# Attention scores of two heads on the two row halves of the array, heads built without doubled rows, weighted sums one block behind

## The chip, the cores and the metric

One Trainium2 core runs the whole program. The metric is device time in microseconds (us): the median of three runs of the kernel before is 1206.73 us (1206.26 to 1209.43).

## What is computed

A hybrid decoder layer on 1024 tokens of width 1024, all in float32. Half of the mixer's width is attention: 8 heads of 64 with RMS-normed queries and keys, three dilated causal windows whose outputs are merged by their softmax denominators. The other half is an S5 state-space mixer with a gated output. Both are normed, projected, added to `x`, and followed by a squared-ReLU MLP of width 4096.

```python
q = _rmsnorm(q, q_norm_g); k = _rmsnorm(k, k_norm_g)
attn = _dilated_attention(q, k, v).reshape(b, s, ATTN_WIDTH)   # 3 windows, merged
ssm = _s5_mixer(u, ...)
mix = concat([_rmsnorm(attn, attn_out_norm_g), _rmsnorm(ssm, ssm_out_norm_g)])
x = x + mix @ w_out
return x + square(relu(_rmsnorm(x, norm2_g) @ w_mlp_up)) @ w_mlp_down
```

The three windows are one softmax here: `bias` (128x1024) adds 8 ln(n) to a score that n windows see, and -1e30 to one that none sees.

## The kernel before, in words

TensorE multiplies fp32r operands. To keep float32 accuracy every operand is held as a rounded high part and the rest as a low part (`split`, L97; `split_scaled`, L101: ACT rounds, DVE subtracts), and a product is a sum of three: high by high, high by low, low by high (`mm3`, L120).

The program runs in this order. `project(0)` and `project(1)` (L219) make the rows of q and k, woven with the state-space mixer (`ssm_params`, `ssm_tables`, `ssm_main`) by the list at L674. Then come the values (`project(2)`), attention over 4 pairs of heads, the gate (`glu`, L712) and the mixer's half of the output projection (`out_ssm`, L786), all woven; then attention's half of the output projection (L834 on), and the MLP (`up_proj`, `down_proj`).

Places that the change and the steps below touch:

- `project` (L219): a row tile of q or k is 128 tokens by 8 heads by 2 copies of 64. ACT takes it from PSUM (L244), squares it into the place of the second copy (L245), DVE sums (L247), POOL forms the reciprocal root (L94, L95), DVE scales (L226), POOL makes the second copy (L227), and POOL's queue writes both copies to DRAM (`d_qk`, L228). Three such tiles rotate.
- `heads(p)` (L518) builds the operands of the pair p: it loads blocks of 512 tokens by 256 columns (`qk_r`, L525), transposes four 128x128 tiles per head and block (`pst`, L539) and evicts them. With the copies doubled, a transposed tile has the head's 64 rows twice, on partitions 0 to 63 and 64 to 127. For k the upper copy becomes the low part (L543, L544); for q the high part (`Qd[0]`) and the low part (`Qd[1]`) are each held twice.
- `scores(i, h)` (L567) takes query blocks 2i and 2i+1 of one head. Each block and each edge of at most 512 keys is two full-array products (L580), q high and q low against the stacked k, so it sums four terms. DVE adds the bias and takes the minimum (L582), ACT exponentiates (L585), DVE and POOL normalise (L587, L588).
- `weigh(i, h, P)` (L592) transposes the weights (`psp`, L603), splits them (`pt`, L606) and multiplies by the values (`mix`, L611). It runs one step behind the scores inside a pair; at a pair's end the last one runs without scores beside it (L647).
- `attn` (L564) yields costs, and `weave` (L649) interleaves two generators by the share of their stated totals; its other stream is `project(2)`, `glu`, `out_ssm` and the next pair's `heads`. What the weave emits is then scheduled, so that every engine has a fixed order.
- PSUM: three banks `s` (scores and `pst`), two `tr`, two `mm`, one `po`. One rotation of two SBUF buffers (`raw`) carries `qk_r`, `v_r`, the gate's and the output projection's weights.

Of the kernel before, what the change touches and what calls it, by code (L numbers as in the profile page):

```python
# [34 lines left out]
def hybrid_layer_kernel(ctx: ExitStack, tc: tile.TileContext, io: dict, out: bass.AP):  # L35
# [47 lines left out]
    d_qk = [dram.tile([T, 1024], F32, name=f"d_{n}") for n in "qk"]  # L83
# [89 lines left out]
    def kv_tiles(p):  # L173
        k, v, q0, q1 = (0, 1, 4, 5) if p % 2 else (6, 7, 8, 9)
        return (place(k, [128, 2, T], F32R, "K2"), [place(q, [128, 2, T], F32R, "Qd") for q in (q0, q1)],
                place(v, [128, 8, 2, 128], F32R, "V2"))
# [42 lines left out]
    def project(c):  # L219
# [3 lines left out]
        def scale(t, row, f):  # L223

            v, dup = row[:, :, 0], row[:, :, 1]
            tc.keep_in_program_order(DVE.tensor_tensor(v, v, f[:, :, None].to_broadcast([128, 8, 64]), op=OP.mult))  # L226
            POOL.tensor_scalar(dup, v, 1.0, 1.0, op0=OP.mult, op1=OP.mult)  # L227
            POOL.dma_start(out=d_qk[c][t * 128:(t + 1) * 128, :], in_=row.rearrange("p h a e -> p (h a e)"))  # L228

        w = [load_w(f"wq{c}_{i}", io["w_qkv"][c, :, 2 * i:2 * i + 2, :], 2, 512, g1, 2 * i) for i in range(4)]  # L230
        for t in ORDER[c]:
# [9 lines left out]
            if c < 2:  # L241
                row = sp2.tile([128, 8, 2, 64], F32, tag="rows", name="rows", bufs=3)
                v, sq = row[:, :, 0], row[:, :, 1]
# [274 lines left out]
    def heads(p, out_):  # L518
# [3 lines left out]
        def load():  # L522
            hf, c = todo.pop(0)
            st = rawp.tile([128, 1024], F32, tag="raw", name="qk_r").rearrange("p (t h e) -> p t h e", t=4, h=2)
            nc.sync.dma_start(out=st.rearrange("p t h e -> p t (h e)"),  # L525
                              in_=d_qk[c][hf * 512:hf * 512 + 512, 256 * p:256 * p + 256].rearrange("(t m) c -> m t c", m=128))
            return hf, c, st
# [3 lines left out]
        K2, Qd, V2 = kv_tiles(p)  # L531
        out_.update(K2=K2, Qd=Qd, V2=V2)
# [31 lines left out]
    def attn(p, K2, Qd, V2, rows=range(4)):  # L564
# [27 lines left out]
        def weigh(i, h, P):  # L592
# [42 lines left out]
            if h == 0:  # L635
                return
# [512 lines left out]
```

## Time and profile before

| what | value |
|---|---|
| median of three runs | 1206.73 us |
| the profiled execution's own time | 1207.53 us |
| its span | 1205.8 us |
| PE busy, of the span | 1131.7 us, 94% |
| DVE, ACT, POOL busy | 819.1, 574.9, 286.2 us |
| mean granted TensorE clock | 0.979 |

PE is TensorE's matmuls, PEld its weight loads. A busy share says only that an engine had something in it. What an engine waited for stands with the idle time ahead of an instruction, and the chain of waits follows the program back from its last instruction. A granted clock of 1.00 is 2.4 GHz, and 0.83 over 10 us means that a third of it ran at 1.2 GHz.

### The profile page before, as it was taken

To read this page: it belongs to the slowest core of one execution; us is meant where nothing else is said; L and a number is where in the kernel's file an instruction comes from. 1 tells how busy PE (TensorE), PEld (TensorE's weight loads), DVE (VectorE), ACT (ScalarE), POOL (GpSimd) and SP (SyncE) were. 2 spreads that over 40 slices of the span, in tenths; PEclk is the share of its full clock that TensorE was granted. 3 is DMA by queue.
4 is the path that set the end of the run, shared out by engine and by line. 5 is a ranking of instruction groups with operands and counts; after the bars stand their busy time and mean duration, and the time that the engine had idled before them with its cause. 6 is when DMAs were issued, how large, how long until landed. Compare 5 with 4: busy or idle time off the path is not lost.

```text
span 1205.8 us, 16171 instructions
## 1 busy us (share of the span) xinstructions
PE 1131.7 (94%) x5720; PEld 931.6 (77%) x5720; DVE 819.1 (68%) x1522; ACT 574.9 (48%) x979; POOL 286.2 (24%) x435
## 2 busy tenths in 40 slices
PE   5978989998999799999899999999999999999998
PEld 4756767787887587887778888888887888888887
DVE  6788886436787677767876666666656775576763
ACT  5432333445677456644555555555553434333332
POOL 4126654411344234333111212111110000000000
PEclk9989899999998899999899999999999999999999
DMA  7843262733433244454354434444399999566930
GB/s 266 330 144 92 90 230 108 249 114 100 141 124 114 94 148 152 141 168 158 122 185 160 159 139 162 155 155 150 123 344 396 386 387 344 190 229 197 324 142 35
DMA packets 112176, 224.49 MB, mean 186 GB/s; under 512 B 9440, under 2 KB 40160, under 8 KB 111072
## 3 DMA queue, kind: packets, MB, share of 16 engines
q1 hardware_dynamic: 92352, 157.31, 39.1%
q0 software_dynamic: 16576, 59.22, 12.8%
q10 hardware_dynamic: 3168, 6.93, 1.5%
q8 instruction: 45, 0.74, 0.2%
q14 instruction: 35, 0.29, 0.1%
HBM read 157.92 MB, written 65.50 MB: 185 GB/s over the span
## 4 chain that ended last, share of the span: by engine, by line
PE 69%; DVE 10%; DMA 10%; ACT 5%; POOL 3%; issue 2%; ACTq 0%; POOLq 0%; DVEq 0%; SPq 0%
PE psy L52 21%; PE psx L52 21%; PE pso L52 8%; PE psq L52 6%; PE psz L52 3%; PE pss L52 2%; PE psp L55 2%; DMA wm<-in_w_up_dram 2%; PE psg L52 2%; DMA wo_r<-in_w_o_dram 1%; PE psn L52 1%; POOL rsq L94 1%; DMA wq_r<-in_w_qkv_dram 1%; PE pst L55 1%; DMA raw<-in_w_down_dram 1%
## 5 line engine op out<-in xcount | busy, mean ns | idle before, releaser
L98 ACT ACTIVATE ud<-raw 128x1024 fp32r<-128x1024 f32 x112 | 112.9, 1053 | 186.0 <-PE psy L52 81.0
L99 DVE TENSOR_TENSOR ud<-raw,ud 128x1024 fp32r<-128x1024 f32 x112 | 132.6, 1221 | 80.2 <-ACT ud L98 80.2
L52 PE MATMUL psx<-X,wu 128*128 128x512 f32 (+1 forms) x780 | 183.0, 386 | 0.0
L52 PE MATMUL psy<-ud 128*128 128x512 f32 x768 | 174.6, 389 | 0.0
L52 PEld LDWEIGHTS psx<-X,wu 128*128 128x128 f32 x780 | 144.7, 188 | 30.2 <-DVE st L938 0.7
L52 PEld LDWEIGHTS psy<-ud 128*128 128x128 f32 x768 | 144.2, 188 | 29.9
L52 PE MATMUL psq<-wq,xt 128*128 128x512 f32 x576 | 146.9, 405 | 0.0
L52 PE MATMUL psx<-ud 128*128 128x512 f32 x576 | 131.5, 389 | 1.1 <-DVE ud L99 1.1
L52 PEld LDWEIGHTS psx<-ud 128*128 128x128 f32 x576 | 108.1, 188 | 23.9 <-DVE ud L99 1.6
L52 PEld LDWEIGHTS psq<-wq,xt 128*128 128x128 f32 x576 | 107.8, 193 | 23.0 <-issue 1.0
L52 PE MATMUL pso<-wo,mt 128*128 128x512 f32 x384 | 104.7, 413 | 5.1 <-ACT wo L102 3.4
L99 DVE TENSOR_TENSOR wu<-wm,wu 128x512 fp32r<-128x512 f32 x112 | 73.7, 687 | 30.4 <-ACT wu L98 30.3
L52 PE MATMUL psy<-X,wu 128*128 128x512 f32 x384 | 92.7, 389 | 0.6 <-ACT st L930 0.6
L98 ACT ACTIVATE wu<-wm 128x512 fp32r<-128x512 f32 x112 | 66.5, 626 | 53.0 <-DMA wm<-in_w_up_dram 26.3
L52 PEld LDWEIGHTS pso<-wo,mt 128*128 128x128 f32 x384 | 72.0, 196 | 21.6 <-ACT wo L102 4.6
L52 PEld LDWEIGHTS psy<-X,wu 128*128 128x128 f32 x384 | 71.8, 188 | 15.8 <-ACT st L930 1.0
L934 POOL DMA_DIRECT2D d_a<-st x80 | 43.2, 540 | 141.7 <-ACT st L940 70.7
L1039 DVE TENSOR_TENSOR raw<-raw 128x1024 f32<-128x1024 f32 x40 | 48.6, 1222 | 32.5 <-DMA raw<-in_w_down_dram 32.5
L588 POOL TENSOR_SCALAR s<-s,dn 128x128 f32<-128x128 f32 (+3 forms) x64 | 50.8, 796 | 70.0 <-DVE dn L587 64.0
L99 DVE TENSOR_TENSOR pt<-psp,pt 128x128 fp32r<-128x128 f32 (+2 forms) x96 | 51.3, 551 | 15.3 <-ACT pt L98 14.7
L52 PE MATMUL pso<-pt,V 128*128 128x256 f32 x320 | 57.6, 303 | 2.9 <-ACT pt L98 2.4
L52 PE MATMUL psu<-wu,xt 128*128 128x512 f32 x192 | 46.9, 404 | 12.3 <-ACT wu L102 8.1
(254 smaller groups left out, 1787.3 us busy)
## 6 DMA issues: line engine op xcount, KB each, us to landing
raw<-in_w_down_dram SPq DMA_DIRECT2D x96, 512.0 KB, 9.0
raw<-d_a SPq DMA_DIRECT2D x56, 512.0 KB, 7.8
d_a<-st POOLq DMA_DIRECT2D x80, 256.0 KB, 2.5
wm<-in_w_up_dram SPq DMA_DIRECT2D x32, 512.0 KB, 3.7
d_x<-x POOLq DMA_DIRECT2D x32, 256.0 KB, 2.6
d_a<-o POOLq DMA_DIRECT2D x32, 256.0 KB, 2.8
wq_r<-in_w_qkv_dram SPq DMA_DIRECT2D x12, 512.0 KB, 4.6
xr<-in_x_t_dram SPq DMA_DIRECT2D x8, 512.0 KB, 4.8
```

What stands on the lines that cost most here:

```text
L52: self.queued(nc.tensor.matmul(*a, **k))
L55: self.queued(nc.tensor.transpose(*a, **k))
L94: POOL.tensor_scalar(v[:, :n], in_, mul, EPS, op0=OP.mult, op1=OP.add)
L98: ACT.activation(h, src, AF.Copy)
L99: eng.tensor_tensor(l, src, h.bitcast(F32), op=OP.subtract)
L588: POOL.tensor_scalar(s[:, :n], s[:, :n], dn, 1.0, op0=OP.mult, op1=OP.mult)
L934: POOL.dma_start(out=d_a[blk // 2][i][blk % 2], in_=st)
L1039: DVE.tensor_tensor(rb, rb, raw_unit(wd(n, *b1)), op=op)
```

## The change

Rows of q and k are written to DRAM once, and POOL's copy is gone. `heads` loads 128 columns of a pair: a transposed tile then has head 0 on partitions 0 to 63 and head 1 on 64 to 127, and one `split_scaled` gives the high and low parts of both. A score product contracts over 64 partitions and uses one half of the array's rows; the two heads' products are issued in turn, into two PSUM banks, three for each head (high by high, high by low, low by high; low by low is gone). `scores` and `weigh` treat both heads of a row i; `weigh` runs a row behind, also across pairs (`carry`), and the pieces of the two are interleaved (`zipped`). Weights of the two heads rotate through four buffers in place of two, and a pair's heads wait until the pair before the last is over.

```diff
-    d_qk = [dram.tile([T, 1024], F32, name=f"d_{n}") for n in "qk"]
+    d_qk = [dram.tile([T, 512], F32, name=f"d_{n}") for n in "qk"]
...
-            v, dup = row[:, :, 0], row[:, :, 1]
+            v = row[:, 0]
             tc.keep_in_program_order(DVE.tensor_tensor(v, v, f[:, :, None].to_broadcast([128, 8, 64]), op=OP.mult))
-            POOL.tensor_scalar(dup, v, 1.0, 1.0, op0=OP.mult, op1=OP.mult)
-            POOL.dma_start(out=d_qk[c][t * 128:(t + 1) * 128, :], in_=row.rearrange("p h a e -> p (h a e)"))
+            POOL.dma_start(out=d_qk[c][t * 128:(t + 1) * 128, :], in_=v.rearrange("p h e -> p (h e)"))
...
-            for h in range(2):
-                pt = s_bank("pst")
-                for t in range(4):
-                    PE.transpose(pt[:, t * 128:t * 128 + 128], st[:, t, h], ident)
-                if c == 0:
-                    split_scaled(Qd[0][:, h, tt], Qd[1][:, h, tt], pt, gqk[:, 0:1])
-                else:
-                    ACT.activation(K2[:, h, tt], pt, AF.Copy, scale=gqk[:, 1:2])
-                    DVE.scalar_tensor_tensor(K2[64:128, h, tt], pt[64:128], gqk[64:128, 1:2],
-                                             K2[64:128, h, tt].bitcast(F32), op0=OP.mult, op1=OP.subtract)
+            pt = s_bank("pst")
+            for t in range(4):
+                PE.transpose(pt[:, t * 128:t * 128 + 128], st[:, t], ident)
+            to = K2 if c else Q2
+            split_scaled(to[:, 0, tt], to[:, 1, tt], pt, gqk[:, c:c + 1])
...
-                    ps = s_bank("pss")
-                    cw = max(256, c1 - c0)
-                    for a in range(2):
-                        PE.matmul(ps[:, :cw], lhsT=Qd[a][:, h, b * 128:(b + 1) * 128],
-                                  rhs=K2[:, h, c0:c0 + cw], start=a == 0, stop=a == 1)
+                ps = [s_bank("pss") for _ in range(2)]
+                cw = max(256, c1 - c0)
+                for aq, ak in ((0, 0), (0, 1), (1, 0)):
+                    for h, hp in enumerate(HALF):
+                        PE.matmul(ps[h][:, :cw], lhsT=Q2[hp, aq, b * 128:(b + 1) * 128], rhs=K2[hp, ak, c0:c0 + cw],
+                                  start=aq + ak == 0, stop=aq == 1)
...
+        for k0 in range(0, nb, 4):
+            kn = min(4, nb - k0)
+            for h in range(2):
+                pt = turn(k0, kn, h)
+                yield kn * 0.22
                 if pend:
                     mix(*pend)
-                    yield pend[1] * 0.213
-                pend = (k0, kn, pt)
+                    yield pend[1] * 0.238
+                pend = (k0, kn, h, pt)
...
         for i in rows:
-            for h in range(2):
-                P, cost = scores(i, h)
-                yield cost
-                if pend:
-                    yield from weigh(*pend)
-                pend = (i, h, P)
-        yield from weigh(*pend)
+            P = [place_turn((9, 0, 13, 14), [128, 2, T], F32, "s") for _ in range(2)]
+            yield from zipped(scores(i, P, K2, Q2), weigh(*carry.pop()) if carry else iter(()))
+            carry.append((p, i, P, V2))
```

The order on the engines, at three places.

PE, inside the rows 2 and 3 of the first pair of heads, before (`pss` scores, two products each):

```order
L52 MATMUL pss_2695<-K2_2217,Qd_2218 128x512
L52 MATMUL pss_2695<-K2_2217,Qd_2219 128x512
L52 MATMUL pss_2699<-K2_2217,Qd_2218 128x256
L52 MATMUL pss_2699<-K2_2217,Qd_2219 128x256
L52 MATMUL pss_2741<-K2_2217,Qd_2218 128x512
L52 MATMUL pss_2741<-K2_2217,Qd_2219 128x512
```

The same place of the changed kernel; here `pss_2701`, `pss_2745`, `pss_2776` are head 0 and `pss_2702`, `pss_2746`, `pss_2777` head 1 (`psp` and `pst` are transposes and `psg` products of the gate, all over the full array):

```order
L52 MATMUL pss_2701<-K2_2201,Q2_2202 128x512
L52 MATMUL pss_2702<-K2_2201,Q2_2202 128x512
L55 MATMUL psp_2812<-pack_66,s_2577 128x128 x4
L55 MATMUL pst_2721<-pack_66,qk_r_2575 128x128 x4
L52 MATMUL pss_2745<-K2_2201,Q2_2202 128x256 x3
L52 MATMUL pss_2746<-K2_2201,Q2_2202 128x256 x3
L52 MATMUL pss_2776<-K2_2201,Q2_2202 128x512 x3
L52 MATMUL psg_2608<-zs_2604,wg0_2593 128x256 x2
L52 MATMUL psg_2730<-zs_2604,wg0_2593 128x256 x2
L52 MATMUL pss_2777<-K2_2201,Q2_2202 128x512 x3
```

The scheduler has kept the two heads in turn for one group and drawn them apart in the next two, and full-array work stands between groups of half-array work. Through the whole order of the changed kernel, the 288 score products stand in 59 unbroken groups (36 of them of six); 117 times a product of one head is followed at once by one of the other, and 54 products have no such partner. Of the 59 groups 4 stand before the last product of the values' projection, 32 between it and the first product of the mixer's output weights, 23 behind that. By width the 117 are 56 of 512, 18 of 384 and 43 of 256 columns, the 54 are 31, 12 and 11.

PE at the first load of a pair, during the values' projection, before and after:

```order
L52 MATMUL psq<-wq_0_2172,xt 128x512 x6
L52 MATMUL psq<-wq_1_2179,xt 128x512 x6
L52 MATMUL psq<-wq_2_2186,xt 128x512 x6
L55 MATMUL pst<-pack,qk_r 128x128 x4
L52 MATMUL psq<-wq_3_2193,xt 128x512 x6
```

```order
L52 MATMUL psq<-wq_0_2156,xt 128x512 x6
L52 MATMUL psq<-wq_1_2163,xt 128x512 x6
L52 MATMUL psq<-wq_2_2170,xt 128x512 x2
L55 MATMUL pst<-pack,qk_r 128x128 x4
L52 MATMUL psq<-wq_2_2170,xt 128x512 x4
L52 MATMUL psq<-wq_3_2177,xt 128x512 x6
```

The first transposes of loaded rows stand four products earlier.

POOL in the first projection, before and after (`f` is a row's scale, `rows` its tile, `U` and `ga` belong to the state-space mixer):

```order
L94 TENSOR_SCALAR rsq<-f 128x8
L95 TENSOR_TENSOR f<-rsq,mhalf 128x8
L227 TENSOR_SCALAR rows<-rows 128x8x64
L228 DMA d_q<-rows 128x1024
L266 TENSOR_SCALAR U_1561<-U_1561 128x1024
L498 TENSOR_SCALAR ga<-ga 128x512 x2
```

```order
L94 TENSOR_SCALAR rsq<-f 128x8
L95 TENSOR_TENSOR f<-rsq,mhalf 128x8
L228 DMA d_q<-rows 128x512
L266 TENSOR_SCALAR U_1554<-U_1554 128x1024
L498 TENSOR_SCALAR ga<-ga 128x512 x2
```

The copy is gone and the write is half as wide; nothing else has moved.

## Rows read from the trace of the kernel before

**Rows 1.** Busy time by stretch, 95 to 515 us of the span: stretch, length, then busy us (instructions) of PE, PEld, DVE, ACT, POOL, the granted clock, the DMA share and GB/s.

```profile
95.00:229.50 134.50, 120.40 (x757) 95.66 (x757) 107.75 (x204) 48.92 (x74) 80.72 (x81) 0.97 0.41 137
229.50:283.00 53.50, 53.48 (x271) 44.97 (x272) 18.75 (x48) 21.27 (x47) 7.69 (x15) 0.97 0.40 139
283.00:396.00 113.00, 102.20 (x675) 88.26 (x675) 89.80 (x234) 78.08 (x174) 42.38 (x67) 0.94 0.39 125
396.00:415.00 19.00, 12.04 (x45) 7.22 (x44) 11.54 (x29) 9.95 (x21) 3.99 (x5) 0.87 0.35 111
415.00:515.00 100.00, 96.37 (x570) 81.19 (x569) 71.83 (x178) 57.57 (x120) 37.03 (x64) 0.99 0.45 143
```

**Rows 2.** What PE's weight loads waited for, 229.5 to 513.6 us: the waiting operation, who released it, us in total, times, longest.

```profile
PEld pso L52 <- ACT pt L98: 7.1, 16, 1.2
PEld psp L55 <- POOL s L588: 6.2, 11, 1.1
PEld pss L52 <- DVE mn L582: 5.5, 12, 0.9
PEld psp L55 <- DVE pt L99: 5.3, 7, 1.8
```

**Rows 3.** PE in order of time, runs of one kind: start us, us until the last one's end, engine, line, what, array rows*columns, shape, count.

```profile
129.47 7.10 PE L52 MATMUL psq<-wq,xt 128*128 128x512 f32 x30
136.41 0.61 PE L52 MATMUL psy<-D,U 128*128 128x128 f32 x4
...
310.39 1.60 PE L52 MATMUL pso<-pt,V 128*128 128x256 f32 x12
311.83 1.60 PE L52 MATMUL psg<-zs,wg 128*128 128x256 f32 x12
313.27 1.09 PE L52 MATMUL pss<-K,Qd 128*128 128x512 f32 x4
...
492.47 1.04 PE L55 MATMUL psp<-pack,s 128*128 128x128 f32 x8
```

**Rows 4.** The transposes of loaded rows and their evictions by tile (`pst`), whole span: duration in ns as least/median/most, first and last start, and how many of each shape.

```profile
L55 PE MATMUL pst<-pack,qk_r x128: 270/272/447, 229.5 to 452.5; 128*128 128x128 f32 x128
L102 ACT ACTIVATE Qd<-pst,pack x16: 677/687/702, 230.6 to 450.7; 128x512 fp32r<-128x512 f32 x16
L103 DVE SCALAR_TENSOR_TENSOR Qd<-pst,pack,Qd x16: 734/751/753, 231.4 to 451.6; 128x512 fp32r<-128x512 f32 x16
```

**Rows 5.** The score products and their evictions by tile (`pss`), whole span; columns as in Rows 4.

```profile
L52 PE MATMUL pss<-K,Qd x192: 274/390/775, 252.4 to 499.7; 128*128 128x512 f32 x96, 128*128 128x256 f32 x64, 128*128 128x384 f32 x32
```

**Rows 6.** First, from the order of time (columns as in Rows 3), the weight loads of one group of the state-space mixer's half-array products (`psy<-ec,X`, 64 rows); then their durations by tile, 136 to 143 us (columns as in Rows 4).

```profile
139.88 0.52 PEld L52 LDWEIGHTS psy<-ec,X 64*128 64x128 f32 x8
...
L52 PEld LDWEIGHTS psy<-ec,X x32: 182/186/188, 137.1 to 142.8; 64*128 64x128 f32 x32
L52 PE MATMUL psy<-ec,X x32: 272/272/373, 137.1 to 142.9; 64*128 64x128 f32 x32
```

**Rows 7.** PE in order of time where half-array products (64*128, `psy<-ec,X`, the two halves in turn) stand between full-array ones; columns as in Rows 3.

```profile
137.12 0.49 PE L52 MATMUL psy<-ec,X 64*128 64x128 f32 x4
137.55 1.19 PE L52 MATMUL psq<-wq,xt 128*128 128x512 f32 x4
138.82 0.49 PE L52 MATMUL psy<-ec,X 64*128 64x128 f32 x4
139.24 0.71 PE L52 MATMUL psy<-D,U 128*128 128x128 f32 x4
139.88 0.72 PE L52 MATMUL psy<-ec,X 64*128 64x128 f32 x8
140.53 0.71 PE L52 MATMUL psy<-D,U 128*128 128x128 f32 x4
141.17 0.71 PE L52 MATMUL psy<-ec,X 64*128 64x128 f32 x8
141.81 0.71 PE L52 MATMUL psy<-D,U 128*128 128x128 f32 x4
```

**Rows 8.** What the DMA queue of SP waited for, 200 to 520 us; columns as in Rows 2.

```profile
SPq L794 <- DMA d_mix<-at: 24.3, 4, 10.6
SPq L112 <- DMA wo_r<-in_w_o_dram: 10.7, 3, 4.2
```

**Rows 9.** What PE waited for, 95 to 230 us; columns as in Rows 2.

```profile
PE psbt L55 <- ACT bt L418: 6.9, 2, 3.7
PE pst L55 <- DMA qk_r<-d_q: 3.0, 1, 3.0
```

**Rows 10.** The chain of waits through the first projection: start us, us, what.

```profile
147.94 1.67 POOL f L95
149.61 0.60 POOL rows L227
150.21 0.28 issue
150.50 2.97 DMA d_q<-rows
...
153.58 0.69 ACT rows L244
...
155.42 0.49 ACT bt L418
...
155.96 0.66 PE psbt L55 x4
...
222.42 6.96 DMA qk_r<-d_q
```

**Rows 11.** Transfers by line, whole span: what, queue, count, KB each, median us from issue to landing.

```profile
d_x<-x POOLq DMA_DIRECT2D x32, 256.0 KB, 2.6
...
qk_r<-d_q SPq DMA_DIRECT2D x8, 512.0 KB, 4.5
...
mx<-d_mix SPq DMA_DIRECT2D x16, 256.0 KB, 3.0
```

More of the change, by code (lines that the diff above doesn't have):

```diff
@@ L173, in kv_tiles @@
     def kv_tiles(p):
[L174 to L175 removed]
+        k, v, q = (1, 4, 5) if p % 2 else (6, 7, 8)
+        return (place(k, [128, 2, T], F32R, "K2"), place(q, [128, 2, T], F32R, "Q2"),
                 place(v, [128, 8, 2, 128], F32R, "V2"))
@@ L530, in heads @@
         yield 0.01
-        K2, Qd, V2 = kv_tiles(p)
-        out_.update(K2=K2, Qd=Qd, V2=V2)
+        while p - 2 not in over:
+            yield 0.05
+        K2, Q2, V2 = kv_tiles(p)
+        out_.update(K2=K2, Q2=Q2, V2=V2)
         while loaded:
@@ new lines, in weigh, with turn, mix @@
+    def weigh(p, i, P, V2):
+        nb = 2 * (i + 1)
+        po = po_bank("pso").rearrange("p (h m) -> p h m", h=2)
+        at, tm = part("x2", [128, 256], "at"), part("xs", [128, 256], "tm")
+        def turn(k0, kn, h):
+            pt = place_turn((10, 11, 12), [128, 2, 4, 256], F32R, "pt")
+            for j in range(2):
+                vb = min(kn, 2 * i + j + 1 - k0)
+                ps = tr_bank("psp")
+                for kb in range(vb):
+                    PE.transpose(ps[:, kb * 128:(kb + 1) * 128], P[h][:, j, (k0 + kb) * 128:(k0 + kb + 1) * 128], ident)
+                pv = ps[:, :vb * 128].rearrange("p (k m) -> p k m", m=128)
+                split(pt[:, 0, :vb, j * 128:j * 128 + 128], pt[:, 1, :vb, j * 128:j * 128 + 128], pv)
+                if vb < kn:
+                    POOL.memset(pt[:, :, vb, j * 128:j * 128 + 128].bitcast(F32), 0.0)
+            return pt
+        def mix(k0, kn, h, pt):
+            for a in range(2):
+                for kb in range(kn):
+                    PE.matmul(po[:, h], lhsT=V2[:, k0 + kb, h, :], rhs=pt[:, a, kb, :], start=k0 + kb + a + h == 0,
+                              stop=k0 + kb == nb - 1 and a == 1, skip_group_check=True)
+            if k0 + kn == nb:
+                hi = HALF[h]
+                ACT.activation(tm[hi], po[HALF[1 - h], h], AF.Copy)
+                DVE.tensor_tensor(at[hi], po[hi, h], tm[hi], op=OP.add)
+        pend = None
+        for k0 in range(0, nb, 4):
+            kn = min(4, nb - k0)
+            for h in range(2):
+                pt = turn(k0, kn, h)
+                yield kn * 0.22
@@ new lines, in weigh, with zipped, attn @@
+        mix(*pend)
+        POOL.dma_start(out=d_mix[0][p, :, 256 * i:256 * i + 256], in_=at)
+        if i == 3:
+            over.add(p)
+        yield pend[1] * 0.238
+    def zipped(x, y):
+        live = [x, y]
+        while live:
+            for z in list(live):
+                w = next(z, None)
+                if w is None:
+                    live.remove(z)
+                else:
+                    yield w
+    def attn(p, K2, Q2, V2, rows=range(4)):
+        for i in rows:
+            P = [place_turn((9, 0, 13, 14), [128, 2, T], F32, "s") for _ in range(2)]
+            yield from zipped(scores(i, P, K2, Q2), weigh(*carry.pop()) if carry else iter(()))
+            carry.append((p, i, P, V2))
```

123 lines of the change are left out of this document (38 added, 85 removed).

## The prediction

> **What bounds the kernel now.** I read the share of each engine first, then busy time by stretch, then what PE waited for, and last PE's instructions in order of time. PE is busy for 94% of the span, so it is its own order and its pauses that count. The change touches two places: the first projection, and attention with what is woven into it. In the table by stretch [rows 1] look at the difference between the length and PE's busy time. The values' projection (229.5 to 283 us) has none: PE has work throughout. From 283 to 396 us PE is idle for 113.0 - 102.2 = 10.8 us while DVE is busy for 89.8 of 113. From 396 to 415 us it is idle for 7.0 us, behind four weight loads that pass through one buffer one after the other. From 415 to 515 us only 3.6 us are idle. The clock column adds to this: 0.94 and 0.87 mean 0.06 x 113 + 0.13 x 19 = 9.3 us lost at 1.2 GHz, after such pauses. The waits have names [rows 2]: weights that POOL has not normalised (6.2 us), transposed weights that ACT and DVE have not split (7.1 and 5.3), score banks that DVE has not emptied (5.5).
>
> **What a PE instruction costs.** Start to start, 30 products of 512 columns take 136.41 - 129.47 = 6.94 us, 0.231 each; 12 of 256 columns take 311.83 - 310.39 = 1.44 us, 0.12 each, and the next 12 the same; eight transposes take (1.04 - 0.27) / 7 = 0.11 each [rows 3, 4]. For 384 columns I take the middle, 0.175. That work changes kind in those rows at no visible price.
>
> **Scores, as counted.** Before: 96, 32 and 64 products of 512, 384 and 256 columns [rows 5], 22.2 + 5.6 + 7.7 = 35.5 us. After there are 288, over half the rows. Whether two halves run side by side is shown where the state-space mixer does it: eight weight loads of half products take 0.52 us, so (0.52 - 0.19) / 3 = 0.11 us for each two [rows 6], which is what one full product of 128 columns takes. I take a pair as one slot. The order does not keep all pairs: 117 pairs and 54 singles are 171 slots, 87, 30 and 54 by width, 20.1 + 5.3 + 6.5 = 31.9 us. **The term is -3.6.** Its bounds: all paired, 26.6 us, -8.9; none side by side, 53.2 us, +17.7.
>
> **The price of changing between half and full.** This decides the sign. Where groups of four full products (128 columns) and eight half products alternate, they start at 139.24, 139.88, 140.53, 141.17 and 141.81 us: 0.64 each [rows 7]. Four slots of 0.11 are 0.44; so 0.20 us is lost at every change, in both directions. With four 512-column products between two groups of four halves, 138.82 - 137.12 = 1.70 us hold 0.22 + 0.92 of work and two changes, so at most 0.28 each. The weight load of the first product behind a change is not hidden: the half products there last 373 ns in place of 272 [rows 6]. The Trainium skill (TensorEngine Tiling (Array Packing), Key Properties) says that a change of the tiling mode drains TensorE, and the trace agrees, with those 0.20 us; the same page's table of speedups (up to 2x for 64 rows) has no price for it, and by that table alone the scores would be worth -8.9 and the changes nothing. The order has 59 groups of half products among full work, 118 changes: **+23.6 us of PE time**. Bounds: 0, if every change falls where PE would wait anyway, and 118 x 0.28 = +33. I take 0.20, which four neighbouring rows give alike.
>
> **Heads.** 64 of 128 transposes go, **-7.0 us** at 0.11. So do 16 evictions on ACT (0.69 us each) and 16 on DVE (0.75) [rows 4]: 11 and 12 us on engines that are not full. They are worth something only through the waits below.
>
> PE's work so grows by 23.6 - 3.6 - 7.0 = **+13.0 us**.
>
> **The waits.** The weights of a row are now transposed a whole row after they were scored, and across pairs; POOL has finished them long before. Of those 6.2 us I take -5 (bounds 0 and -6.2). In `weigh` the transposes of one head now stand between those of the other and its products, so ACT and DVE have one more piece of time, and less to do: half of 7.1 + 5.3, -6 (bounds 0 and -12.4). Score groups now want two of three banks at once, which DVE empties in turn; this can double the 5.5 us or, with other work between, take it away; I take 0 (bounds -5.5 and +5.5). A third of the lost clock returns with the pauses, -3 (0 to -5). Part of the changes falls into what is left of the idle time: 32 of the 59 groups lie between the values' projection and the first product of the mixer's output weights, where PE has pauses, 27 where it has next to none. I take -3 (0 to -8). **Sum: -17.**
>
> Beside this, the tile that collects both heads' output is reserved at the start of a row, not after the first head, and rotates with the residual's loads, whose queue already waits 24.3 us for it [rows 8]. None of that shows among PE's waits, so it is 0, with +5 as the far end. The four weight loads behind the pause at 396 us keep their order and, one behind the other [rows 8], their buffer: 0.
>
> **The first projection.** Twice PE waits some 3.5 us for ACT, together 6.9 us [rows 9]. The chain there runs [rows 10]: POOL's root, its copy (0.60 and 0.28 until the issue), the write (2.97), ACT's next row, ACT's `bt`, PE. The copy goes, 0.9 us, and the write halves; writes of 256 KB take 2.6 us elsewhere [rows 11], so another 0.4. Twice 1.3 is **-2.6** (bounds 0, if ACT is late for another reason, and -3.5). The first load of `qk_r` took 6.96 us [rows 10] and held PE for 3.0 [rows 9]. With half the bytes it may be 2 us shorter (loads of 256 KB take 3.0 us against 4.5 for these 512 KB [rows 11]); but its transposes stand four products, 0.9 us, earlier in the order: **-1.1** (0 to -3). The other copies and writes of rows are hidden behind PE's products, and nothing of theirs is on the chain.
>
> **Sum.** +13.0 - 17 - 2.6 - 1.1 = -7.7. Against the profiled execution's own 1207.5 us that is 1199.8; this execution lies 0.8 above the median of the three runs, so I forecast a median of **1199**. About 0.3%, 3.6 us, is what a measurement of this kernel can tell from no change, so "faster" is below 1203.1 and "slower" above 1210.3.
>
> **The rivals.**
>
> *Bare changes, slower.* The price of 0.20 us is paid at all 118 places, and the waits stay, because in the stretches where 27 groups lie there is no idle time to fill, and in the other DVE at 80% sets the pace as before. Then 13.0 - 3.7 = +9.3: 1216. It decides as soon as the waits return less than 5.7 of the 17. For it speaks how evenly the 0.64 us repeat [rows 7]; the skill's rule on draining, named above, is the same mechanism. Against it, that more than half of the groups lie where PE waits. Chance 0.23.
>
> *The halves do not stream at once.* With 128 columns the weight loads could hide that two products take turns. With 512 they could not: +17.7 in place of -3.6, 21 us more than forecast, 1220. Against it, the weight loads themselves do overlap [rows 6], and nothing in the rows shows the streams taking turns. Chance 0.05.
>
> *The waits all but vanish.* All 18.6 us for POOL, ACT and DVE go [rows 2], with 5 us of clock and the 3 hidden: 13.0 - 26.6 - 3.7 = -17.3, 1189. For it, the deeper pipeline and 23 us less on ACT and DVE. Against it, 59 new breaks in PE's stream, each of which holds an eviction back. Chance 0.19.
>
> *A draw.* The same terms, with the waits returning 6 to 13 us: 1203 to 1210, no difference that can be told. Chance 0.20. The forecast itself, 1193 to 1203, has 0.33.
>
> **How the numbers follow.** Faster is the forecast and the vanishing waits, 0.52. Same is the draw with a little of its neighbours, 0.21. Slower is 0.27: bare changes, halves in turn, less what of the first ends under 1210. For 8 in 10 the range must take in most of the rivals on both sides: 1186 to 1218. Below it lie perhaps 0.07, above it 0.10.
>
> **What would show it.** Two half products of 512 columns start some nanoseconds apart, and the next two 0.23 us later. Around a group of halves PE loses 0.2 us at each side. POOL vanishes from what the transposes of the weights wait for; the wait for ACT before `psbt` falls by 2 to 3 us; PE's idle time from 283 to 415 us falls from 17.8 to about 10. Wrong it would be if the changes cost much less with fp32r products of 512 columns than with the 128-column ones seen here, or if the score groups' need of two banks made DVE the pace of the whole stretch; a stretch from 283 to 396 us with DVE above 90% would say so.

## The result, and the profile after

The changed kernel took 1192.69 us in the median of 4 runs, the one before 1207.40 in 4 runs on the same chip: a ratio of 0.9877, 95% interval 0.9853 to 0.9900. Measured once more beside three experiments it took 1194.72 (6 runs), the one before 1204.46 (10 runs): 0.9909, 0.9884 to 0.9934. An eleventh run of the one before, at a granted clock of 0.584, took 1770.29 us and is left out. So the change is worth 10 to 15 us, faster by about 1%. The forecast was 1199, a gain of 7.7; the direction was right and the time lies in the range, the size was too small.

The profiled execution of the changed kernel took 1194.41 us, span 1192.6. Busy time by stretch, the stretches set at the same places of the program as in [rows 1] (first projection, values' projection, attention up to the first output weights, their loads, the rest); columns as there:

```profile
93.00:221.00 128.00, 118.55 (x756) 94.53 (x754) 103.27 (x204) 49.02 (x74) 70.54 (x67) 0.98 0.37 115
221.00:271.20 50.20, 50.20 (x232) 39.92 (x231) 11.72 (x32) 15.52 (x35) 5.59 (x11) 0.94 0.35 116
271.20:372.00 100.80, 94.84 (x653) 77.52 (x651) 74.17 (x188) 69.40 (x151) 37.29 (x60) 0.95 0.37 117
372.00:390.00 18.00, 15.79 (x62) 10.39 (x59) 10.33 (x27) 8.35 (x20) 4.66 (x8) 0.72 0.28 87
390.00:503.00 113.00, 108.20 (x647) 85.37 (x647) 79.04 (x192) 64.70 (x139) 41.72 (x71) 0.97 0.39 124
```

Two things stand out against [rows 1]. The first line is 6.5 us shorter, and VectorE is busy 4.5 us less in it; PE's work there is the same (757 and 756 instructions). From the third and fourth line PE's idle time is 6.0 + 2.2 = 8.2 us, where it was 17.8. The clock has not come back: length times what the granted clock lacks to 1.00, summed over the five lines, is 19 us, and was 16 before (PE's pauses included).

What PE's weight loads waited for, 221 to 503 us (columns as in [rows 2]):

```profile
PEld pss L52 <- issue: 6.5, 26, 0.4
PEld psp L55 <- DVE pt L99: 5.8, 12, 1.8
...
PEld psp L55 <- POOL s L589: 4.5, 7, 1.4
...
PEld pso L52 <- DVE at L619: 2.8, 5, 1.3
PEld pso L52 <- ACT pt L98: 2.6, 7, 0.5
...
PEld pss L52 <- DVE mn L579: 1.4, 6, 0.4
```

Against [rows 2], the wait for ACT's `pt` fell by 4.5 us and that for VectorE's emptying of score banks by 4.1; POOL's normalising is still waited for, 4.5 us in place of 6.2. New is `at`: both heads' sums share one bank, and the next row's first sum waits until it is read, 2.8 us. New too is the first line, "issue", idle time that nothing in the profile ends: it stands ahead of score products, and the full array below has none of it there. It is the weight loads' idle time and not PE's: ahead of the `pso` at 302.53 us below they are idle for 0.37 us while the half products still run. What PE itself waited for in the first projection, 93 to 221 us (columns as in [rows 9]):

```profile
PE pst L55 <- DMA qk_r<-d_q: 2.8, 1, 2.8
PE psbt L55 <- ACT bt L418: 2.2, 1, 2.2
PE psbt L55 <- DVE bj L133: 2.0, 1, 2.0
```

The wait for `bt` fell from 6.9 to 2.2 us, a new one of 2.0 for VectorE's `bj` stands in one of its places, and the first `qk_r` is waited for as before. A third wait of the kernel before, which stands in the view of [rows 9] below the lines shown there, is gone:

```profile
PE psb L52 <- DVE z L503: 1.6, 1, 1.6
```

Now the price of a change between full and half products, from PE in order of time (columns as in [rows 3]):

```profile
300.04 1.67 PE L52 MATMUL psg<-zs,wg 128*128 128x256 f32 x12
301.64 0.96 PE L52 MATMUL pss<-K,Q 64*128 64x512 f32 x6
302.53 1.21 PE L52 MATMUL pso<-pt,V 128*128 128x256 f32 x8
303.74 1.69 PE L52 MATMUL psg<-zs,wg 128*128 128x256 f32 x12
305.36 0.96 PE L52 MATMUL pss<-K,Q 64*128 64x512 f32 x6
306.25 0.33 PE L55 MATMUL psp<-pack,s 128*128 128x128 f32 x1
```

Six half products of 512 columns take 302.53 - 301.64 = 0.89 us until the next full one: three slots of 0.231 and 0.20. Two of them start 1 to 4 ns apart, and the third two follow the second two after 0.23 us. By single starts a change shows twice. The last `psg` and the first half product start 0.21 us apart in place of 0.12, so 0.09 is lost at the change; the next start loses 0.10 more (0.33 in place of 0.23). Behind the group it is the same, 0.32 in place of 0.23 and then 0.22 in place of 0.12. The 0.89 us hold the second half of the change in front and the first half of the one behind. So each side costs 0.2 us, as [rows 7] had it at 128 columns: wherever nothing else is waited for, 0.19 to 0.20 in front of and behind groups of 256, 384 and 512 columns, 0.15 where transposes follow.

To place the gain, three stretches between products that every version has: from the last product of `psu` (57.8 us in the changed kernel, 59.2 before) to the last transpose `pszt`, which ends the mixer; from there to the first `psz`, attention with all that is woven into it; and the rest. They are taken between the ends of these products. In brackets each is cut in three: PE's idle time; what the slow clock took from its busy time (half of the busy time at 1.2 GHz); and what is left, its busy time at full clock.

| | POOL copies rows | mixer, us (idle, slow clock, busy) | attention, us (idle, slow clock, busy) |
|---|---|---|---|
| before | yes | 155.0 (21.1, 5.5, 128.4) | 371.5 (32.2, 15.2, 324.2) |
| after | no | 148.8 (16.3, 4.1, 128.4) | 365.7 (23.2, 17.9, 324.6) |
| after, second measurement | no | 149.4 (16.8, 4.3, 128.4) | 365.2 (24.5, 16.5, 324.3) |

Length and PE's busy time stand first in these lines, the granted clock behind POOL's; mixer before and after, then attention before and after:

```profile
59.20:214.20 155.00, 133.89 (x894) 106.16 (x894) 130.31 (x244) 54.31 (x87) 79.39 (x80) 0.94 0.41 131
57.80:206.60 148.80, 132.50 (x894) 105.41 (x894) 126.13 (x243) 53.77 (x87) 70.59 (x68) 0.97 0.38 115
214.20:585.80 371.60, 339.39 (x1930) 283.09 (x1929) 250.37 (x582) 209.81 (x446) 128.55 (x215) 0.96 0.44 145
206.60:572.40 365.80, 342.59 (x1962) 273.19 (x1961) 232.90 (x534) 201.06 (x430) 125.00 (x211) 0.95 0.41 133
```

The last part hardly moves: in the mixer it is 128.2 to 129.1 us in all versions, in the attention of the six profiles that share the changed one 324.3 to 326.5, while their slow clock takes 10.6 to 17.9 and their stretch 361.7 to 365.7. So a difference of 3 us in the stretch can be the clock's.

So about 6 us come from each. In the mixer 4.3 to 4.8 of them are PE's idle time; in attention 7.7 to 9.0 us of idle time went, and the slow clock took 1.3 to 2.7 back. The remaining 1.4 us lie ahead of the projection, where both programs hold the same instructions; what they are is open.

### The profile page after: what moved, and what is told of

Same layout as the page of the kernel before. It is cut to its first block, busy times and chain, and to the rows that moved or that the text cites. A ratio compares the mean times of both kernels' runs of the same rounds, so it can differ in the third digit from the quotient of the medians.

```text
span 1192.6 us, 16170 instructions
## 1 busy us (share of the span) xinstructions
PE 1135.3 (95%) x5752; PEld 923.5 (77%) x5752; DVE 798.3 (67%) x1474; ACT 566.3 (47%) x963; POOL 274.1 (23%) x419
## 4 chain that ended last, share of the span: by engine, by line
PE 73%; DVE 11%; DMA 8%; POOL 3%; ACT 3%; issue 2%; SPq 0%; POOLq 0%; ACTq 0%; DVEq 0%
PE psx L52 24%; PE psy L52 22%; PE pso L52 7%; PE psq L52 6%; PE psz L52 4%; PE pss L52 3%; PE psp L55 2%; PE psg L52 2%; POOL rsq L94 1%; DMA raw<-in_w_down_dram 1%; DMA wo_r<-in_w_o_dram 1%; DMA wq_r<-in_w_qkv_dram 1%; PE psn L52 1%; DMA U<-d_u 1%; DVE bw L469 1%
## 5 line engine op out<-in xcount | busy, mean ns | idle before, releaser
L52 PEld LDWEIGHTS psy<-X,wu 128*128 128x128 f32 x384 | 71.8, 188 | 15.1 <-ACT st L929 0.3
L589 POOL TENSOR_SCALAR s<-s,dn 128x128 f32<-128x128 f32 (+7 forms) x64 | 49.6, 786 | 76.2 <-DVE dn L587 75.7
L98 ACT ACTIVATE pt<-psp 128x128 fp32r<-128x128 f32 (+2 forms) x96 | 44.2, 486 | 35.1 <-PE psp L55 34.6
```

The source lines that it names most:

```text
L52: self.queued(nc.tensor.matmul(*a, **k))
L98: ACT.activation(h, src, AF.Copy)
L589: POOL.tensor_scalar(s[h][:, :n], s[h][:, :n], dn[:, h:h + 1], 1.0, op0=OP.mult, op1=OP.mult)
```

## The experiments: the first projection

**Rows alone.** The kernel before, with only the copy and the doubled half of the write gone; the doubling moves to the load.

```diff
-            POOL.tensor_scalar(dup, v, 1.0, 1.0, op0=OP.mult, op1=OP.mult)
-            POOL.dma_start(out=d_qk[c][...], in_=row.rearrange("p h a e -> p (h a e)"))
+            POOL.dma_start(out=d_qk[c][...], in_=v.rearrange("p h e -> p (h e)"))
...
+            for h in range(2):
+                for a in range(2):
+                    nc.sync.dma_start(out=st[:, :, h, 64 * a:64 * a + 64], in_=d_qk[c][...])
```

> The kernel before with the first projection's part of the change alone: POOL's copy of each row and the doubled half of its write are gone, and the doubling moves into the load of the heads, as four strided transfers in place of one. Attention is left as it was. Theory A (the copy and the half write on the chain to PE's waits at 121 and 156 us, and the 1.2 GHz that follows such a wait, are worth more than the 2.6 us of the prediction, as the trace of the changed kernel looks, where the last product of the mixer starts 7.7 us earlier and 1.9 of that is there before the projection begins): 1207 - 5 to 6 = 1201 to 1202. Theory B (only the 2.6 us that the prediction gave; the rest was a draw of the clock): 1204 to 1205. Theory C (the projection's gain in the changed kernel is a draw altogether, and the four transfers cost on SP): 1207 or more.

Measured: 1200.22, ratio 0.9963 (0.9944 to 0.9981); mixer 147.7 us (16.7, 2.3, 128.7), attention 371.3. The mixer's stretch gains 7.3 us, 4.4 of idle time and 3.2 of slow clock; attention gains nothing. In the time 4.3 of it show, between theories A and B; the stretch says A.

**Rows back.** The changed kernel with copy and wide write restored.

```diff
+            POOL.tensor_scalar(row[:, 1], v, 1.0, 1.0, op0=OP.mult, op1=OP.mult)
-            POOL.dma_start(out=d_qk[c][...], in_=v.rearrange("p h e -> p (h e)"))
+            POOL.dma_start(out=d_qk[c][...], in_=row.rearrange("p a h e -> p (a h e)"))
```

> The changed kernel with the first projection's part undone: POOL copies each row again and writes rows of 512 KB; the heads read the half that they need, as in the changed kernel. Theory A: the gain of the projection goes, +5 to +6 us on 1192.7, 1198 to 1199. Theory B: +2.6, 1195. Theory C: no difference, 1192 to 1193.

Measured: 1196.68, ratio 0.9931 (0.9903 to 0.9958); mixer 154.1 (20.9, 4.9, 128.2), attention 362.9. The loss of 5 us in the mixer is there. Then the copy and the width of the write, each by itself:

```diff
# copy alone: the copy is made and written, 256 KB
+            POOL.tensor_scalar(row[:, 1], v, 1.0, 1.0, op0=OP.mult, op1=OP.mult)
+            POOL.dma_start(out=d_qk[c][...], in_=row[:, 1].rearrange("p h e -> p (h e)"))
# write alone: no copy, 512 KB
+            POOL.dma_start(out=d_qk[c][...], in_=row.rearrange("p a h e -> p (a h e)"))
```

> The changed kernel, with POOL's copy of each row back on the way to the write, but the write still 256 KB and the heads unchanged. What the mixer's end (last transposed output) takes from the end of the first products is 148.8 us in the changed kernel and 155.0 in the one before. Theory A (the copy does it, in two ways: 0.9 us on the chain at each of two places, and on VectorE, whose two-operand instructions that run beside a POOL copy take 1.10 us in place of 0.68 in the trace of before, 8 of them, 3.4 us): 152 to 155, and +4 to +5 us in the time, 1197 to 1198. Theory B (the width of the write does it, through the buffers of the rows that ACT waits for, 11.5 us before and 8.3 after): 149, and no difference in the time.

> The changed kernel with writes of rows of 512 KB again (the second half holds the squares, which nobody reads), without POOL's copy. Theory A: from the first products' end to the mixer's end 149 to 150 us, and +0 to +1 us in the time, 1193 to 1194. Theory B: 153 to 155, and +4 to +6, 1197 to 1199.

Measured: copy alone 1195.33, ratio 0.9933 (0.9908 to 0.9957), mixer 154.0 (21.3, 4.2, 128.4); write alone 1193.13, ratio 0.9924 (0.9901 to 0.9948), mixer 149.8 (17.0, 4.4, 128.4). The times differ too little to tell them apart; the stretch does. It takes 154.0 to 155.0 us in the three profiles with the copy and 146.8 to 149.8 in all others that keep POOL's remaining work. The idle time is clearer still: 20.9 to 21.3 us with the copy, 16.3 to 17.0 without it. The copy does it; the wide write by itself makes 0.2 to 0.7. Copy alone, then write alone, in the mixer's stretch:

```profile
57.80:211.80 154.00, 132.74 (x894) 105.42 (x895) 129.81 (x244) 54.36 (x87) 79.73 (x80) 0.96 0.36 111
57.90:207.70 149.80, 132.81 (x894) 105.40 (x894) 126.53 (x244) 54.32 (x87) 71.41 (x68) 0.95 0.42 136
```

What PE waited for ahead of `psbt`, copy alone (two lines) and write alone:

```profile
PE psbt L55 <- ACT bt L419: 3.1, 1, 3.1
PE psbt L55 <- DVE bj L133: 2.9, 1, 2.9
PE psbt L55 <- ACT bt L418: 5.1, 2, 2.8
```

So at these two waits, 4.2 us in the changed kernel and 6.9 before, the copy puts back 1.8 and the wide write 0.9. The rest of what the copy costs stands elsewhere: with the copy alone the wait for `z` ahead of `psb` is back too, 1.9 us, with the wide write alone it is not. How a copy can do that is seen on VectorE in the kernel before (in order of time; start, us, engine, line, what):

```profile
115.26 1.11 DVE L226 TENSOR_TENSOR rows<-rows,f 128x512 f32<-128x512 f32 x1 [0.65 <-POOL f L95]
116.29 2.09 DVE L131 TENSOR_TENSOR s<-rpow,bb 128x512 f32<-128x512 f32 x1
118.31 1.10 DVE L132 TENSOR_TENSOR s<-rpow,bb 128x512 f32<-128x512 f32 x1
```

POOL in the same microseconds (a kernel's line numbers are its own):

```profile
115.22 0.61 POOL L227 TENSOR_SCALAR rows<-rows 128x512 f32<-128x512 f32 x1
116.13 0.62 POOL L228 DMA_DIRECT2D d_q<-rows  x1 [0.30 <-DMA D<-d_kz]
116.78 1.06 POOL L266 TENSOR_SCALAR U<-U 128x1024 f32<-128x1024 f32 x1
117.91 1.97 POOL L498 TENSOR_SCALAR ga<-ga 128x512 f32<-128x512 f32 x2
```

and in the changed kernel:

```profile
113.30 0.69 DVE L227 TENSOR_TENSOR rows<-rows,f 128x512 f32<-128x512 f32 x1 [0.65 <-POOL f L95]
113.91 1.59 DVE L131 TENSOR_TENSOR s<-rpow,bb 128x512 f32<-128x512 f32 x1
115.42 1.10 DVE L132 TENSOR_TENSOR s<-rpow,bb 128x512 f32<-128x512 f32 x1
```

With two operands in SBUF and 512 elements a partition such a product takes 0.68 us alone; beside POOL's copy it takes 1.11, beside the regrouping of `U` and the scaling ahead of the tanh more. From the end of the first products to 230 us there are 13 VectorE instructions in the kernel before that last over 0.2 us longer than the least of their kind, every one of them beside elementwise work of POOL, and together they lose 7.1 us. In the changed kernel there are 4, and they lose 2.6. These products stand in front of `bj`, the transposes to `psbt` and so PE; up to the mixer's end it is 6.3 us before and 2.6 after, 3.7 less, where PE's idle time fell by 4.3 to 4.8. How much of that fall is VectorE's lost time and how much the copy's own place in the chain to the row's write, no run separates. The Trainium skill (SBUF — State Buffer, Who interferes with whom) says that a VectorE instruction with two SBUF inputs contends with a GpSimd instruction that reads SBUF; the trace agrees, with 0.43 us lost to a copy of 0.61. In the copy-alone run the pair reads 1.11 and 2.10 again:

```profile
114.31 1.11 DVE L227 TENSOR_TENSOR rows<-rows,f 128x512 f32<-128x512 f32 x1 [0.65 <-POOL f L95]
115.34 2.10 DVE L131 TENSOR_TENSOR s<-rpow,bb 128x512 f32<-128x512 f32 x1
```

**POOL quiet.** If that is the cause, the 2.6 us that are left can be had as well.

```diff
-        POOL.tensor_scalar(ug, ur.rearrange("p t (g c) -> p g t c", g=8), 1.0, 1.0, op0=OP.mult, op1=OP.mult)
+        ACT.activation(ug, ur.rearrange("p t (g c) -> p g t c", g=8), AF.Copy)
...
-            POOL.tensor_scalar(ga, ga, GELU_C, 1.0, op0=OP.mult, op1=OP.add)
+            ACT.activation(ga, ga, AF.Copy, scale=GELU_C, bias=1.0)
```

> The changed kernel with the last two elementwise operations of POOL that run beside the mixer moved to ACT: the regrouping of U (1.1 us each on POOL, 4 of them) and the scaling ahead of the tanh (0.79, 8 of them). In the trace of the changed kernel four VectorE products run beside them and take 1.10 to 1.59 us in place of 0.68, 2.6 us in all, in front of the transposes that PE waits for. Theory A (what the undoubled rows returned was VectorE's time beside POOL): the stretch of the mixer falls by a further 2 to 3 us, to 145 to 147, and the time by as much, ratio to before 0.2 per cent lower than that of the changed kernel. Theory B (the rows returned it through the chain of the write alone, and ACT now has 10 us more to do): no difference or up to 2 us slower.

Measured: 1184.69, ratio 0.9835 (0.9809 to 0.9861), faster than the kernel before and than the changed one beside it (0.9909). The same three products, and the mixer's stretch:

```profile
112.44 0.69 DVE L227 TENSOR_TENSOR rows<-rows,f 128x512 f32<-128x512 f32 x1 [0.65 <-POOL f L95]
113.05 0.69 DVE L131 TENSOR_TENSOR s<-rpow,bb 128x512 f32<-128x512 f32 x1
113.65 0.68 DVE L132 TENSOR_TENSOR s<-rpow,bb 128x512 f32<-128x512 f32 x1
```

```profile
57.90:203.30 145.40, 131.84 (x894) 104.69 (x895) 123.64 (x244) 61.02 (x99) 61.85 (x55) 0.96 0.38 118
```

The mixer's stretch is 145.4 us (13.6, 2.8, 129.1), 2.5 below the mean of 147.9 over the nine profiles with single rows and narrow writes; PE's idle time there, 16.3 to 16.8 in the nine, is 2.7 to 3.2 lower. That was expected. The two operations also left POOL's queue and run on another engine, and what that alone is worth was not tried. The time fell by 10 us in the median, which was not expected: the granted clock was 0.987 in the median of its runs and 0.9795 in those of the changed kernel, and at the 0.8 us for each 0.001 that the last section shows, that is an estimated 6 us more. Why this version's clock is higher is open.

## The experiments: attention

**Full array.** What the changes between half and full cost on the path. The sums hold the features of both heads, so this kernel leaves out what the scores are and keeps only their work.

```diff
-                for aq, ak in ((0, 0), (0, 1), (1, 0)):
-                    for h, hp in enumerate(HALF):
-                        PE.matmul(ps[h][:, :cw], lhsT=Q2[hp, aq, ...], rhs=K2[hp, ak, ...], ...)
+                for h in range(2):
+                    for a in range(2):
+                        PE.matmul(ps[h][:, :cw], lhsT=Q2[:, a, ...], rhs=K2[:, h, ...], ...)
```

> The changed kernel with its scores over the whole array: for each head two products of 128 rows in place of three of 64, on the same tiles, so that the features of both heads are in each sum (the values of the scores are others; the number, the widths and the order of all other work stay). Full slots 192 in place of 186 (+0.9 us), and none of the 118 changes between half and full products. Theory A (each change costs PE its 0.20 us, and nearly all of that is on the path): 1192.7 + 0.9 - 23 + some 3 that turn into waits = 1174, within 1171 to 1178. Theory B (the changes fall where PE would wait for DVE or ACT anyway): 1188 to 1193.

Measured: 1179.41, ratio 0.9783 (0.9758 to 0.9808). Attention takes 352.8 us (29.5, 11.9, 311.4), 12 to 13 less than in the two profiles of the changed kernel, 9 to 13 less than in the six that share its attention:

```profile
204.50:557.30 352.80, 323.29 (x1865) 272.34 (x1864) 232.35 (x534) 200.11 (x430) 126.21 (x211) 0.96 0.43 138
```

Neither theory: of 118 x 0.20 = 23 us 9 to 13 are on the path. PE's busy time at full clock falls by 13 to 15 us, and 4 to 7 of these come back as idle time (29.5 in place of 22.9 to 25.6).

**Full array, kept whole.** The same with the heads apart: doubled again, two full products a head, the rest as changed.

```diff
-        k, v, q = (1, 4, 5) if p % 2 else (6, 7, 8)
+        k, v, q0, q1 = (0, 1, 4, 5) if p % 2 else (6, 7, 8, 9)
...
-                PE.transpose(pt[:, t * 128:t * 128 + 128], st[:, t], ident)
+                    PE.transpose(pt[:, t * 128:t * 128 + 128], st[:, t, h], ident)
...
-            P = [place_turn((9, 0, 13, 14), [128, 2, T], F32, "s") for _ in range(2)]
+                P = [place_turn((2, 3, 13, 14), [128, 2, T], F32, "s") for _ in range(2)]
```

> A version that computes the same as both: the changed kernel's rows, its sums one block behind across pairs and its two-head banks, but the heads doubled again (by four strided transfers at the load, 128 transposes, 16 more evictions on ACT and DVE) and the scores as two full products a head. It needs one more 8 KB buffer a pair; weights of the rows take turns in two buffers that the projection of the values has left. Theory A (changes on the path): 1192.7 - 23 + 0.9 + 7.0 of transposes + 2 to 4 for the evictions and what turns into waits = 1180, within 1176 to 1185. Theory B (changes hidden): 1200 or more.

Measured: 1210.18, ratio 1.0049 (1.0027 to 1.0072), attention 379.7 (41.7, 13.6, 324.4). It is 27 us longer there than the full array above, for 64 more transposes (7.0 us), 32 more evictions and another order; among the waits of PE's weight loads POOL's normalising stands first:

```profile
PEld psp L55 <- POOL s L598: 12.1, 9, 3.7
```

Theory B's number, but not its reason, since the full array alone did gain. How much is the doubled heads and how much the order, this run does not separate. What it shows is that the price of the changes is less than what their avoidance costs here.

**No carry.** The sums of a pair's last row drained at its end.

```diff
             carry.append((p, i, P, V2))
+        if rows[-1] == 3:
+            yield from weigh(*carry.pop())
```

> The changed kernel with the sums of a pair's last row drained at the end of the pair, as before, and not carried into the next pair: the rest, the two heads side by side above all, stays. In the order that comes out of it there are 62 groups of halves in place of 59. Theory A (the carry across pairs is worth a good part of what the waits returned: at three ends of pairs the last transposes wait some 1.5 us for POOL's rows and again for ACT and VectorE): +4 to +9 us, 1197 to 1202. Theory B (what returned the waits is that a row's two heads are weighed while the next row is scored, within a pair; its ends have other work): +0 to +3, 1193 to 1196.

Measured: 1197.39, ratio 0.9960 (0.9933 to 0.9987), attention 371.2 (26.0, 18.7, 326.6), as long as in the kernel before. By its number theory A: the carry across pairs is worth 6 to 10 us by the two ratios, 5.5 to 6 by the stretch. But not for its reason, since the waits that it named have not come back:

```profile
PEld psp L55 <- POOL s L589: 5.3, 7, 1.2
PEld pso L52 <- ACT mt L98: 4.7, 2, 4.4
PEld psp L55 <- DVE pt L99: 3.4, 8, 0.9
...
PEld pss L52 <- DVE mn L579: 2.4, 6, 0.9
...
PEld pso L52 <- ACT pt L98: 2.2, 5, 0.7
```

The four waits of [rows 2] sum to 13.3 us here, and to 13.4 in the second profile of the changed kernel (5.0, 4.7, 2.5 and 1.2). What differs is a pause ahead of the output projection (`mt`), an order with fewer pairs and more groups (96 pairs, 62 groups; 102 and 59 in the changed kernel), and the slow clock, 18.7 us in place of 17.9 and 16.5. So attention's gain hangs on the carry, but the carry is not what brought those waits down.

**Whole groups.** The first product of a group waits for both banks, and the six are held in turn.

```diff
+                        if one:
+                            after(PE.last, one)
+                        elif emptied.get(n0 - 4):
+                            after(PE.last, emptied[n0 - 4], True)
+                        one = PE.last
```

> The changed kernel with one more rule of order: the first product of a score group waits until both of its banks are empty, and the six follow each other head by head in turn, so that the scheduler no longer issues one head's three products alone. In the order that comes out of it the pairs stay together but for six split groups: 150 slots in place of 186, 114 changes in place of 118. Theory A (PE's slots and changes are what counts): 36 x 0.18 + 4 x 0.20 = 7.3 us less PE work, of which between half (as with the changes taken away) and all shows: 1186 to 1189. Theory B (the groups now wait for VectorE to empty two banks, and the wait takes it back): 1192 or more.

Measured: 1197.93, ratio 0.9953 (0.9931 to 0.9976), attention 372.1 (30.8, 23.7, 317.6). The order came out as wanted, 139 pairs (starts within 50 ns) and 10 single products, where the changed kernel ran 102 and 84. Yet it is no faster than that, rather slower. Compare the attention stretch of the changed kernel's second profile, of this one and of the next (length, then PE's busy time first and the granted clock behind POOL's):

```profile
207.20:572.40 365.20, 340.74 (x1960) 272.28 (x1959) 232.34 (x534) 200.56 (x430) 125.15 (x211) 0.95 0.41 133
```

```profile
206.80:578.90 372.10, 341.29 (x1961) 273.94 (x1961) 232.60 (x534) 200.08 (x430) 124.10 (x211) 0.93 0.40 131
```

```profile
204.90:571.90 367.00, 341.25 (x2025) 273.95 (x2024) 231.80 (x534) 200.84 (x430) 124.31 (x211) 0.97 0.41 132
```

The work did fall, busy time at full clock by 7 to 9 us. But PE idles 30.8 us in place of 24.5, and runs longer at 1.2 GHz. The two banks, as theory B had it, are a part of the waits, 3.3 us in place of 1.2; POOL is the larger, 8.5 in place of 5.0:

```profile
PEld psp L55 <- POOL s L605: 8.5, 7, 2.2
...
PEld pss L52 <- DVE mn L594: 3.3, 11, 0.4
```

**Transposed twice.** 7.0 us of PE work added.

```diff
-            for t in range(4):
-                PE.transpose(pt[:, t * 128:t * 128 + 128], st[:, t], ident)
+            for _ in range(2):
+                for t in range(4):
+                    PE.transpose(pt[:, t * 128:t * 128 + 128], st[:, t], ident)
```

> The changed kernel with each of the 64 transposes of the heads issued twice into the same bank: 64 x 0.11 = 7.0 us more on PE, nothing else changed, the term that the prediction took for the transposes with its sign turned. Theory A (on the path in full): +7 us. Theory B (half of it or less shows, the rest falls into waits): 0 to +4.

Measured: 1194.53, ratio 0.9923 (0.9906 to 0.9940), within 0.2 us of the changed kernel. The third line above shows where the 7 us went: the stretch is only 1.8 us longer and the clock 0.97 in place of 0.95. By its number theory B, but the waits took in nothing: attention is 367.0 us (25.8, 8.6, 332.7). The added work is there in full, 6 to 8 us more busy time at full clock, the idle time is 25.8 in place of 24.5, and the slow clock took 8.6 us in place of 16.5.

**Head by head.** Three products of one head ahead of the other's.

```diff
-                for aq, ak in ((0, 0), (0, 1), (1, 0)):
-                    for h, hp in enumerate(HALF):
+                for h, hp in enumerate(HALF):
+                    for aq, ak in ((0, 0), (0, 1), (1, 0)):
```

> The changed kernel with the three products of one head ahead of the three of the other: the row groups can then stream side by side only where one head's last meets the other's first. Some 240 slots in place of 186, 54 x 0.18 = 9.9 us more on PE (18.7 if nothing pairs); as many changes as before (59 groups). Theory A (PE's slots are on the path): +7 to +12 us, ratio to before 0.6 to 1.0 per cent higher. Theory B (attention goes by its waits, as the kept groups suggested, which took 7 us of slots away and were not faster): within 3 us of the changed kernel, and less idle time of PE instead.

Measured: 1188.49, ratio 0.9875 (0.9853 to 0.9896). It did not try what it meant to: the scheduler put the heads in turn again, 113 pairs ran where 102 did in the changed kernel beside it. That an almost equal order reads 0.9875 against 0.9909, with intervals that overlap, says how finely orders can be told apart here. What one head after the other would cost was not tried.

**The second measure.** The changed kernel again; its numbers stand above.

> The changed kernel once more, as the measure for the three others of this call. The first measurement gave 0.9877 of the time of before, from four runs of each. 1190 to 1194 on a chip on which before takes 1204 to 1207; the stretch of the mixer 147 to 150 us, attention 362 to 366 us, as in the five profiles that share this order.

## Why the prediction was right in direction and half as large

*The first projection: a term that held, and what the sum left out.* The -2.6 for the two places came: the waits ahead of `psbt` fell from 6.9 to 4.2 us, and the copy alone put back 1.8 of it, the wide write 0.9, where I gave 1.8 and 0.8. But the stretch gained 5.6 to 6.2 us, 7.3 in the rows alone. The step that failed is "The other copies and writes of rows are hidden behind PE's products, and nothing of theirs is on the chain". A third wait went, 1.6 us for VectorE's `z`, and the slow clock took 1.2 to 1.4 us less from PE's busy time, 3.2 in the rows alone; for neither had the sum a term in this stretch. What was missed is that POOL's copies also slow VectorE, which was busy for 25.35 of the 26 us ahead of the first wait for `bt`. The rows that told it, 1.11 beside 0.68 us for the same instruction, were in the trace of before; I read mean durations and not their spread.

*Attention: the sum right, the terms not.* The forecast for it was -5.1 (the -7.7 without the -2.6), measured -5.8 and -6.3. That it fits is luck, since three misses cancel. As the profile counts busy time, PE's at full clock rose by 0.4 and 0.1 us, where the forecast had +13.0 of work; its idle time fell by 9.0 and 7.7, where the waits without the clock (-14) and the first load (-1.1) made -15.1; the slow clock took 2.7 and 1.3 more, where -3 was given. A wait shorter than the shown tail of a product counts as busy, so this does not say where the 13 went. By terms:

- Changes, 118 x 0.20 = +23.6 with 3 hidden: the count and the price are as read, and they hold at 512 columns. But without them the stretch is only 9 to 13 us shorter; the other 10 or more fall where PE would have paused for something else.
- Scores, -3.6 from 171 slots: the chip ran 102 pairs, 186 slots, -1.0. I had counted pairs in the order; products of one head that stand alone in it broke more of them. The whole groups show that more pairs would not have helped.
- Transposes, -7.0: gone as counted (128 to 64).
- First load, -1.1: the wait for `qk_r` went from 3.0 to 2.8 us.
- Waits, -11 without clock and cover: of the four in [rows 2] 24.1 us became 14.3, with 2.8 new for `at`, so -7.0. Of the causes given, the carry across pairs is not it, since without it they stay at 13.3. That both heads are weighed together, a row behind, is left; no run takes it away, so it is argued, not shown. "POOL vanishes" was wrong: it was waited for 4.5 us. That `at` costs nothing was wrong too, though not by its DMA queue but by its bank.
- Clock, -3: wrong, as above.
- The idle time from 283 to 415 us was to fall to about 10, and fell to 8.2; VectorE did not become the pace (74.17 of 100.80 us).

A sum that fits is not a proof of its terms: 7 us of work on PE could be added for nothing, since the clock gave it back, and 7.7 (37 slots and 4 changes, whole groups) taken away at a loss.

*The rivals.* "Bare changes" fell because the changes are only partly bare. "The halves do not stream at once" fell by the 1 to 4 ns. "The waits all but vanish" comes near in time (1189), but for another reason: half of the gain is the first projection's.

*Left open:* the 1.4 us ahead of the projection; why a version's granted clock is what it is; how the doubled heads' price divides; what brought attention's waits down.

## What to carry to other kernels

Before an operation of POOL is costed at its own time, look at the spread of VectorE's durations: here the instruction with a least time of 0.68 and a most of 1.11 us had a neighbour on POOL, and what that neighbour cost stood on VectorE's chain. Scores on halves of the array paid 0.2 us at each side of every group here, so the number of groups in the order that the scheduler gives counts as much as the products saved. Where PE waits for three engines in turn, test a term by adding it or taking it away, and read idle time and clock apart before you say where it went.

## What the runs showed of the hardware

The scatter between runs of one kernel goes mostly with its granted clock. Of the twelve runs of the whole groups one at 0.970 took 1200.96 us and one at 0.983 took 1190.20, 0.8 us for each 0.001. One run of the doubled transposes falls out of that: at 0.935 it took 1194.31 us, no more than its neighbours at 0.983 to 0.989. Work added to PE can pay for itself that way: the doubled transposes had 0.986 in the median and the changed kernel's time, the changed kernel 0.9795. A change between full and half products costs the same 0.20 us with 256, 384 and 512 columns, so it is not a share of the products at its sides.
